# The attention's query load as two transfers of 64 rows in place of one that reads its source twice

## The chip, the cores and the metric

The kernel runs on one core of one Trainium2 chip. Its time is the device time of one execution in microseconds (us); before the change it is 2788.62 us, the median of three runs (2783.65 to 2796.56). A core has five engines with a queue of instructions each: TensorE (PE, with its weight loads shown apart as PEld), VectorE (DVE), ScalarE (ACT), GpSimd (POOL) and SyncE (SP). Transfers between the core's memory (SBUF) and the device's memory are issued by an engine's queue and carried out by the core's 16 DMA engines. Here SP and POOL issue them: the profile calls SP's transfers hardware_dynamic (q1) and POOL's software_dynamic (q0).

## The reference

One layer of a hybrid decoder is run for a prompt of 2048 tokens behind 16 meta tokens, and for 8 x 8 sample tokens with a paged cache of 512 keys each. One input projection gives q, k and v for 8 heads of width 64 and the inputs of a recurrent branch. Attention weights come from a product over the keys behind a position, taken from the query backwards:

```python
z = jnp.einsum('bqhd,bkhd->bhqk', q, k) * (HEAD_DIM ** -0.5) + bias
mask = k_pos[None, :] < q_pos[:, None]
log_keep = jnp.where(mask, jax.nn.log_sigmoid(-z), 0.0)
suffix = lax.cumsum(log_keep, axis=3, reverse=True) - log_keep
w = jnp.where(mask, jnp.exp(jax.nn.log_sigmoid(z) + suffix), 0.0)
out = jnp.einsum('bhqk,bkhd->bqhd', w, v)
...
mixed = jnp.concatenate([attn, lru * jax.nn.gelu(gate)], axis=-1) @ w_out
x = x + rmsnorm(mixed, g_mix_post)
u = jax.nn.relu(rmsnorm(x, g_mlp_pre) @ w_up)
x = x + rmsnorm((u * u) @ w_down, g_mlp_post)
```

## The kernel before, in words

All values are float32. Each operand of a large matrix product is split into a rounded part and the rest (names with `hi` and `lo`), and a product is the sum of three matrix products: lines L181 to L183 where the weights stand still in the array, L213 to L215 where the activations do. Weights come in tiles of 512 KB (`wraw`, two buffers), loaded by SP (L149) and split by ACT (L158) and DVE (L159).

The prompt is worked in four blocks of 512 tokens (`s` from 0 to 3). First comes the input projection of block 0 with the sample tokens, and then, beside the following input projections, the attention of the sample tokens (`sample_attn`: cache pages are gathered by POOL at L831, PE uses them at L854 and L883). Then the input projections of blocks 1 to 3, and after them the output projection and the MLP of blocks 0 to 3. The prompt's attention (`attn`) is side work that lasts into the MLP of block 2 (PE's last L702 stands at 2126.7 us): a planner (`Work`) cuts it into small steps and puts a few of them on PE's queue after every few matrix products of the main work, by a table of rates. PE's order is written out this way by hand. The other engines' instructions are put in order by a scheduler. Each queue runs in order, so an instruction that waits holds up what stands behind it.

The input projection stores its queries, split, in the device's memory as `qd[s]` with the shape [8 heads, 64, 2, 512] (L604), its keys as `kd` (L550) and its values as `vd` (L556). The attention of block `s` takes the heads one after the other. For each head, `head` loads the queries into the tile `q` (128 partitions, 2 x 512 elements: 4 KB per partition, two buffers). The 64 rows of the head stand in it twice, in partitions 0 to 63 and again in 64 to 127, because the keys beside it hold their rounded part in the upper 64 partitions and the rest in the lower 64. This load is the line L667, issued by POOL. `head` also loads the block's last 128 keys and values (`kvt`, L671 and L672), and `kv_load` the others in groups (`kv`: L684, L685 and L688 for the first group, L691 and L692 for the others). The two buffers of `q` also serve the sample attention's weights (`wt`, L871).

A step of attention is then: logits on PE (L702, from `kv` or `kvt` and `q`), two sigmoids on ACT (L640, L641), a scan and a product on DVE (L645 or L648, L652), transposes on PE (L712), a split on ACT and DVE (L719, L720, L723, L724; for the 16 meta keys POOL clears the tile first at L718), and the product with the values on PE (L734, L736). A head's result is summed into a tile with the tag `pb` (L744, L745) and stored in `md` by SP (L746). The scan's results use the same two `pb` buffers.

POOL's queue holds, besides the loads, the gate's polynomial in the input projection (L524 to L528, L454), small copies for the convolution (L499, L502) and the inverse roots of the norms (L237).

POOL's transfers announce their landing through eight semaphores, DMASW0 to DMASW7, taken in turn. The transfer that takes a semaphore again waits until the transfer eight places earlier has landed.

Of the kernel before, what the change touches and what calls it, by code (L numbers as in the profile page):

```python
# [20 lines left out]
HD = 64  # L21
NMETA = 16
SB = 512
# [61 lines left out]
def _program(tc, I, O, NSB, NSC):  # L85

    nc = tc.nc
# [16 lines left out]
    def T(p, shape, dt, tag, bufs=1):  # L104
        uid[0] += 1
        return p.tile(shape, dt, name=f"{tag}_{uid[0]}", tag=tag, bufs=bufs)
# [162 lines left out]
    qd = [dt([NH, HD, 2, SB], F32, name=f"qd{s}") for s in range(NSB)]  # L269
# [386 lines left out]
    def attn(s, K):  # L656
# [4 lines left out]
        def keys(h, a, n):  # L661
            return kd[h].rearrange("e p n -> (e p) n")[:, a:a + n]

        def head(h):
            if h < NH and h not in heads:
                q = T(att, [P, 2, SB], F32R, "q", 2)
                nc.gpsimd.dma_start(q.rearrange("p e n -> p (e n)"),  # L667
                                    qd[s][h].rearrange("p e n -> p (e n)").unsqueeze(0).to_broadcast([2, HD, 2 * SB]))
                kt = T(att, [P, 256], F32R, "kvt", 3)
                k0 = SB * s + 3 * P  # L670
                nc.gpsimd.dma_start(kt[:, 0:P], keys(h, NMETA + k0, P))  # L671
                nc.gpsimd.dma_start(kt[:, P:2 * P], vd[h, :, k0:k0 + P])  # L672
                live["kvt"] += 1
                heads[h] = {"q": q, "kt": kt, "carry": [None] * 4, "out": None}
            return heads.get(h)
# [72 lines left out]
        def s_items():  # L748

            for n, (h, g) in enumerate(groups):  # L750
                H = head(h)
                if g == s:
                    head(h + 1) if live["kvt"] < 3 else None
                while live["kv"] > 2:
                    yield None
                kv_load(n)
                kv_load(n + 1)
                head(h)
                kvt = kvs.pop(n)
                if g == 0:  # L760
# [533 lines left out]
```

## Time and profile before

| | |
|---|---|
| median of three runs | 2788.62 us (2783.65 to 2796.56) |
| the profiled execution's own time | 2790.22 us |
| its span, first to last instruction | 2788.3 us |
| mean clock granted to PE | 0.985 |
| DVE, ACT, POOL busy | 65%, 52%, 18% of the span |
| bytes moved | 368.23 MB, 132 GB/s |
| by SP's queue and POOL's queue | 287.35 MB and 78.52 MB |

How to read it: a time in a row is counted from the start of the span. "Landing" is the time from the issue of a transfer until its semaphore is complete. In a timeline, a bracket at the end of a row tells how long the engine was idle before it and what ended the wait. The chain of waits is the work that ended last, followed back from the last instruction of the span. The granted clock (PEclk) is 1.00 when PE runs at full speed.

### The profile page before, as it was taken

The page shows a single profiled execution, that of the slowest core. Times are in us where ns is not written, and L with a number is a line of the kernel's source. Part 1 is how long each engine was busy: PE and PEld are TensorE (multiplying, and loading weights), DVE is VectorE, ACT ScalarE, POOL GpSimd, SP SyncE. Part 2 cuts the span into 40 slices and gives each one's busy share as a digit, 9 for nine tenths or more (in the row PEclk, how much of TensorE's full clock was granted, in tenths as well). Part 3 has the DMA queues.
Part 4 walks back from the last instruction along what each step waited for, and adds up shares of the span by engine and source line. Part 5 has one row for each costly group of instructions (what it writes and reads, how often), then busy time and mean ns, then how long its engine had stood idle before and what let it go on. Part 6 is the DMA issues. An engine that isn't in the chain of part 4 may idle for free.

```text
span 2788.3 us, 36998 instructions
## 1 busy us (share of the span) xinstructions
PE 2688.2 (96%) x13804; PEld 2219.4 (80%) x13804; DVE 1814.3 (65%) x2790; ACT 1451.6 (52%) x2426; POOL 515.5 (18%) x711
## 2 busy tenths in 40 slices
PE   8999988998899999999999999999999999999998
PEld 6886766777688888887788888878888887998996
DVE  5456364686777777788867777798686436433434
ACT  6556364575665655565555555665555234332332
POOL 5336361341211101112110001120000002000002
PEclk9999998999999999999999999999999999999999
DMA  4465855467534433345443333454333334322223
GB/s 161 134 208 189 261 152 171 134 169 221 166 92 128 119 115 106 106 138 154 154 110 115 103 111 103 138 162 143 105 96 104 112 119 144 99 84 77 83 84 113
DMA packets 177316, 368.23 MB, mean 132 GB/s; under 512 B 49153, under 2 KB 79361, under 8 KB 177137
## 3 DMA queue, kind: packets, MB, share of 16 engines
q1 hardware_dynamic: 103792, 287.35, 32.2%
q0 software_dynamic: 73344, 78.52, 11.3%
q8 instruction: 109, 1.79, 0.3%
q14 instruction: 71, 0.57, 0.1%
HBM read 305.51 MB, written 60.04 MB: 131 GB/s over the span
## 4 chain that ended last, share of the span: by engine, by line
PE 80%; DVE 7%; DMA 5%; POOL 3%; issue 3%; ACT 2%; SPq 0%; POOLq 0%; DVEq 0%; ACTq 0%
PE D L181 11%; PE D L183 11%; PE D L182 11%; PE D L213 10%; PE D L214 10%; PE D L215 10%; PE T L712 4%; PE T L702 4%; PE O L734 2%; PE O L736 2%; DVE wlo L159 1%; DMA md<-pb 1%; DVE pb L648 1%; POOL rstd L237 1%; DMA q<-qd 1%
## 5 line engine op out<-in xcount | busy, mean ns | idle before, releaser
L159 DVE TENSOR_TENSOR wlo<-wraw,whi 128x1024 fp32r<-128x1024 f32 x368 | 464.2, 1261 | 496.1 <-ACT whi L158 495.8
L181 PE MATMUL D<-ahi,whi 128*128 128x512 f32 (+3 forms) x1920 | 709.2, 369 | 0.0
L183 PE MATMUL D<-ahi,wlo 128*128 128x512 f32 (+3 forms) x1920 | 686.3, 357 | 2.0 <-DVE wlo L159 2.0
L182 PE MATMUL D<-alo,whi 128*128 128x512 f32 (+3 forms) x1920 | 685.0, 357 | 2.8 <-DVE alo L1017 1.5
L158 ACT CAST whi<-wraw 128x1024 fp32r<-128x1024 f32 x368 | 386.6, 1050 | 485.5 <-PE D L214 282.8
L213 PE MATMUL D<-whi,uh 128*128 128x512 f32 x1024 | 418.1, 408 | 0.0
L183 PEld LDWEIGHTS D<-ahi,wlo 128*128 128x128 f32 x1920 | 364.8, 190 | 53.2 <-DVE wlo L159 2.9
L181 PEld LDWEIGHTS D<-ahi,whi 128*128 128x128 f32 x1920 | 365.2, 190 | 51.9 <-issue 8.7
L214 PE MATMUL D<-whi,ul 128*128 128x512 f32 x1024 | 405.2, 396 | 0.0
L215 PE MATMUL D<-wlo,uh 128*128 128x512 f32 x1024 | 404.3, 395 | 0.0
L182 PEld LDWEIGHTS D<-alo,whi 128*128 128x128 f32 x1920 | 365.7, 190 | 45.5 <-DVE alo L1017 1.7
L640 ACT ACTIVATE keep<-T,nbias 128x512 f32<-128x512 f32 (+6 forms) x352 | 209.7, 596 | 241.7 <-PE T L702 234.6
L648 DVE TENSOR_TENSOR_SCAN pb<-keep,carry 128x513 f32<-128x513 f32 (+1 forms) x228 | 270.3, 1186 | 71.9 <-ACT keep L640 69.9
L724 DVE TENSOR_TENSOR wtl<-T,wth 128x512 fp32r<-128x512 f32 (+1 forms) x320 | 191.0, 603 | 73.7 <-ACT wth L723 72.6
L723 ACT CAST wth<-T 128x512 fp32r<-128x512 f32 (+1 forms) x320 | 166.1, 523 | 127.6 <-PE T L712 122.7
L215 PEld LDWEIGHTS D<-wlo,uh 128*128 128x128 f32 x1024 | 192.7, 188 | 46.7
L213 PEld LDWEIGHTS D<-whi,uh 128*128 128x128 f32 x1024 | 192.9, 188 | 39.9 <-DVE uf L1032 0.4
L214 PEld LDWEIGHTS D<-whi,ul 128*128 128x128 f32 x1024 | 193.3, 189 | 38.6
L652 DVE TENSOR_TENSOR beta<-beta,pb 128x512 f32<-128x512 f32 (+7 forms) x360 | 208.2, 578 | 0.0
L641 ACT ACTIVATE beta<-T,bias 128x512 f32<-128x512 f32 (+6 forms) x352 | 208.2, 591 | 0.0
L712 PE MATMUL T<-ident,beta 128*128 128x128 f32 (+1 forms) x1216 | 193.7, 277 | 14.1 <-ACT beta L641 7.6
L702 PE MATMUL T<-kv,q 128*128 128x512 f32 (+5 forms) x640 | 180.4, 364 | 10.3 <-ACT beta L641 4.4
(235 smaller groups left out, 3600.0 us busy)
## 6 DMA issues: line engine op xcount, KB each, us to landing
wraw<-in_w_up SPq DMA_DIRECT2D x128, 512.0 KB, 3.5
wraw<-in_w_down SPq DMA_DIRECT2D x128, 512.0 KB, 3.5
wraw<-in_w_in SPq DMA_DIRECT2D x64, 512.0 KB, 3.9
q<-qd POOLq DMA_DIRECT2D x32, 512.0 KB, 16.9
wraw<-in_w_out SPq DMA_DIRECT2D x32, 512.0 KB, 3.5
kv<-kd POOLq DMA_DIRECT2D x48, 256.0 KB, 4.1
kv<-vd POOLq DMA_DIRECT2D x48, 256.0 KB, 4.2
y<-in_x_prompt SPq DMA_DIRECT2D x16, 512.0 KB, 5.6
```

The costliest lines, as they stand in the source:

```text
L158: nc.scalar.copy(hi, r)
L159: nc.vector.tensor_tensor(lo, r, hi.bitcast(F32), op=ALU.subtract)
L181: nc.tensor.matmul(o, whi[:, k, :], ahi(k, a, b), start=(k == 0), stop=False)
L182: nc.tensor.matmul(o, whi[:, k, :], alo(k, a, b), start=False, stop=False)
L183: nc.tensor.matmul(o, wlo[:, k, :], ahi(k, a, b), start=False, stop=(k == KC - 1))
L213: nc.tensor.matmul(o, h, whi[:, kk, :], start=st, stop=False)
L214: nc.tensor.matmul(o, l, whi[:, kk, :], start=False, stop=False)
L215: nc.tensor.matmul(o, h, wlo[:, kk, :], start=False, stop=sp)
L640: nc.scalar.activation(keep[:, o:512], S, AF.Sigmoid, bias=nbias, scale=-0.125)
L648: nc.vector.tensor_tensor_scan(pb[:, o:513][:, ::-1], kr, kr, 1.0 if carry is None else carry, op0=ALU.mult, op1=ALU.bypass)
L702: nc.tensor.matmul(o, H["q"][:, e, i * P:(i + 1) * P], kap, start=(e == 0), stop=(e == 1))
L712: nc.tensor.transpose(t[0:kn, i * P:(i + 1) * P], w[:, c0:c0 + kn], ident)
```

## The change

The transfer at L667 had a source that names the head's 64 rows of 4 KB twice: a first dimension of 2 with a step of zero, then 64 rows. It is replaced by two transfers (L668) of the same 64 rows each, one into partitions 0 to 63 and one into 64 to 127. The bytes, the tile and its two buffers stay the same. There are 32 heads in all, so 32 transfers of 512 KB become 64 of 256 KB.

```diff
         def head(h):
             if h < NH and h not in heads:
                 q = T(att, [P, 2, SB], F32R, "q", 2)
-                nc.gpsimd.dma_start(q.rearrange("p e n -> p (e n)"),
-                                    qd[s][h].rearrange("p e n -> p (e n)").unsqueeze(0).to_broadcast([2, HD, 2 * SB]))
+                for r in range(2):
+                    nc.gpsimd.dma_start(q[HD * r:HD * r + HD].rearrange("p e n -> p (e n)"), qd[s][h].rearrange("p e n -> p (e n)"))
                 kt = T(att, [P, 256], F32R, "kvt", 3)
```

The orders of PE, DVE, ACT and SP stay as they were, instruction by instruction; only POOL's queue changes. The first place is the first query load of block 0, in the middle of the gate's polynomial and just ahead of the last cache page (L831). In brackets stand the semaphores that a row waits for. Before:

```order
L525 TENSOR_SCALAR gt_3699<-gt_3699 128x512 [waits Pool_49]
L667 DMA q_3925<-qd_78 128x1x1024 [waits DMAHW4_49]
L526 TENSOR_TENSOR gt_3699<-gt_3699,g_3697 128x512 [waits Pool_49]
L528 TENSOR_TENSOR gt_3699<-gt_3699,g_3697 128x512 [waits Activation_49]
L454 TENSOR_TENSOR ii_3765<-ii_3765,xc_3661 128x512 [waits Activation_49]
L831 DMA kv_3835<-in_cache_v,ix_199 128x512 [waits DMASW7_49,DMASW6_49,PE_49]
```

The same place after the change:

```order
L525 TENSOR_SCALAR gt_3699<-gt_3699 128x512 [waits Pool_49]
L668 DMA q_3925<-qd_78 64x1024 [waits DMAHW4_49]
L526 TENSOR_TENSOR gt_3699<-gt_3699,g_3697 128x512 [waits Pool_49]
L668 DMA q_3925<-qd_78 64x1024
L528 TENSOR_TENSOR gt_3699<-gt_3699,g_3697 128x512 [waits Activation_49]
L454 TENSOR_TENSOR ii_3765<-ii_3765,xc_3661 128x512 [waits Activation_49]
L831 DMA kv_3835<-in_cache_v,ix_199 128x512 [waits DMASW7_49,DMASW6_49,PE_49]
```

The second half stands one instruction behind the first, and the cache page stands one instruction later.

The second place is a later head of block 0, on POOL's queue: its query load, its `kvt` and its group of `kv`. Before, seven transfers make a head:

```order
L667 DMA q_5182<-qd_78 128x1x1024 [waits DMASW3_49,PE_49]
L671 DMA kvt_5184<-kd 128x128 [waits DMASW4_49,PE_49]
L684 DMA kv_4833<-kd 128x400 [waits DMASW5_49,PE_49]
L685 DMA kv_4833<-vd 128x384 [waits DMASW6_49]
L686 MEMSET kv_4833 128x128
L672 DMA kvt_5184<-vd 128x128 [waits DMASW7_49]
L688 DMA kv_4833<-vmd 16x128 [waits DMASW0_49,Pool_49]
L688 DMA kv_4833<-vmd 16x128 [waits DMASW1_49]
```

After the change there are eight:

```order
L668 DMA q_5187<-qd_78 64x1024 [waits DMASW0_49,PE_49]
L668 DMA q_5187<-qd_78 64x1024 [waits DMASW1_49]
L671 DMA kvt_5190<-kd 128x128 [waits DMASW2_49,PE_49]
L684 DMA kv_4838<-kd 128x400 [waits DMASW3_49,PE_49]
L685 DMA kv_4838<-vd 128x384 [waits DMASW4_49]
L686 MEMSET kv_4838 128x128
L672 DMA kvt_5190<-vd 128x128 [waits DMASW5_49]
L688 DMA kv_4838<-vmd 16x128 [waits DMASW6_49,Pool_49]
L688 DMA kv_4838<-vmd 16x128 [waits DMASW7_49]
```

With eight transfers to a head, each waits for the semaphore of the same transfer of the head before.

The third place is the only one where two instructions change places, on POOL's queue in an input projection (the copy at 558.30 us of the profile). Before:

```order
L718 MEMSET wth_5101 128x512 [waits PE_49]
L528 TENSOR_TENSOR gt_5043<-gt_5043,g_5041 128x512 [waits Activation_49]
L667 DMA q_5464<-qd_78 128x1x1024 [waits DMAHW7_49,DMASW2_49,PE_49]
L502 COPY convc_240<-xp_5140 128x3 [waits Activation_49]
L454 TENSOR_TENSOR ii_5112<-ii_5112,xc_4994 128x512 [waits Activation_49]
L499 COPY xp_5268<-convc_240 128x3 [waits DVE_49,Pool_49]
```

After:

```order
L718 MEMSET wth_5106 128x512 [waits PE_49]
L528 TENSOR_TENSOR gt_5048<-gt_5048,g_5046 128x512 [waits Activation_49]
L668 DMA q_5470<-qd_78 64x1024 [waits DMAHW7_49,DMASW0_49,PE_49]
L668 DMA q_5470<-qd_78 64x1024 [waits DMASW1_49]
L454 TENSOR_TENSOR ii_5117<-ii_5117,xc_4999 128x512 [waits Activation_49]
L502 COPY convc_240<-xp_5145 128x3
L499 COPY xp_5274<-convc_240 128x3 [waits DVE_49,Pool_49]
```

The product L454 now stands ahead of the small copy L502 there.

## The prediction

> **What bounds the kernel now.** I read the page first, then PE's time by stretches, then who it waited for, then the chain of waits, and last the transfers. The page's first part says that PE is the bound:
>
> ```profile
> PE 2688.2 (96%) x13804; PEld 2219.4 (80%) x13804; DVE 1814.3 (65%) x2790; ACT 1451.6 (52%) x2426; POOL 515.5 (18%) x711
> ```
>
> Some 100 us are left in which PE stands still. The stretches show where (PE busy is the second number, and the last three are granted clock, DMA share and GB/s):
>
> ```profile
> 395.00:800.00 405.00, 354.54 (x1680) 281.70 (x1680) 275.34 (x460) 238.60 (x421) 108.06 (x159) 0.92 0.57 163
> 800.00:2788.00 1988.00, 1961.67 (x9808) 1644.99 (x9806) 1325.02 (x2006) 988.24 (x1651) 216.55 (x338) 1.00 0.38 115
> ```
>
> From 395 to 800 us, where block 0's attention runs beside the input projections and the first output projection, PE idles 50 us and has a clock of 0.92. Behind 800 us it idles 26 us in 1988 at full clock. The query load's line within the first stretch counts 13 of the 32 loads:
>
> ```profile
> L667 POOL DMA_DIRECT2D q<-qd x13: 798/817/911, 401.7 to 765.7; - x13
> ```
>
> So the 19 others run beside a PE that hardly waits. What the change can give lies in the first stretch. PE's waits there, the longest first (total, times, longest):
>
> ```profile
> PE O L883 <- DMA kv<-in_cache_v,ix: 7.7, 1, 7.7
> PE T L712 <- ACT beta L641: 7.6, 2, 4.8
> PE T L702 <- DMA q<-qd: 6.0, 1, 6.0
> ```
>
> One wait names the query load itself. The chain of waits names a transfer as the last releaser in each of these places (start, duration):
>
> ```profile
> 408.55 11.47 DMA kv<-in_cache_v,ix
> 426.47 20.01 DMA q<-qd
> 470.96 12.12 DMA vd<-vst
> 496.57 11.24 DMA md<-pb
> 558.93 8.36 DMA md<-gt
> 621.89 9.47 DMA md<-pb
> 643.25 8.69 DMA out_v_prompt<-sf
> ```
>
> The profile's list of transfers shows that several of these are slow for their kind (KB each, median us to landing):
>
> ```profile
> wraw<-in_w_up SPq DMA_DIRECT2D x128, 512.0 KB, 3.5
> q<-qd POOLq DMA_DIRECT2D x32, 512.0 KB, 16.9
> kv<-kd POOLq DMA_DIRECT2D x48, 256.0 KB, 4.1
> ...
> vd<-vst SPq DMA_DIRECT2D x12, 512.0 KB, 7.8
> ...
> md<-pb SPq DMA_DIRECT2D x32, 128.0 KB, 3.8
> ...
> kv<-in_cache_v,ix POOLq DMA_INDIRECT x32, 5.1
> ```
>
> A query load takes 16.9 us, a weight tile of the same 512 KB 3.5. Why is read from a stretch in which a query load (issued at 514.7) moves almost alone:
>
> ```profile
> 519.00:522.00 3.00, 3.00 (x22) 2.55 (x21) 1.91 (x3) 2.11 (x4) 0.00 (x0) 1.00 0.14 52
> ```
>
> It moves 52 GB/s with a DMA share of 0.14, and 0.14 x 16 is 2.2 engines. At 52 GB/s its 524 KB take 10 us, and the rest of the 16.9 is start, end and company. The old source's first dimension is 2. I take it that a load is shared out over the engines by that dimension, two engines here. So the load is slow itself and, for some 15 us, fills two of the engines that every other transfer needs too. While the load of 462.9 us was in flight, these landed:
>
> ```profile
> vd<-vst SPq DMA_DIRECT2D x2, 512.0 KB, 10.5
> ...
> md<-pb SPq DMA_DIRECT2D x1, 128.0 KB, 11.9
> kvt<-kd POOLq DMA_DIRECT2D x1, 64.0 KB, 12.4
> ```
>
> The `kvt` load, 64 KB, took as long as the rest of the query load ahead of it; the `md` store took three times its median.
>
> **The change part by part.**
>
> *The halves' landing.* No row shows a POOL load of 64 rows. The nearest below is `kv<-kd` with the same 256 KB in 128 rows, 4.1 us; the far end is the old load, 16.9. I take 5 us for both halves (4.1, and the second issued 0.6 us later with some company), since 64 rows are a first dimension like `kv`'s 128, not like the old 2.
>
> The Trainium skill (DMA: Bandwidth & Descriptors, section "Why a DMA increments its semaphore by 16 and not by 1") says that a copy runs on the largest number of engines up to 16 that divides the slowest dimension of both sides: 2 for the old source and 16 for 64 rows. The 0.14 agrees for the old; no run yet shows the new. The same page (section "Anatomy of one DMA") puts a load at about 2.0 us plus bytes over 436 GB/s. By that the old load would be an estimated 3.2 us and two halves 2.6 each, so that splitting would only add a fixed cost and the sum would be nothing; the measured 16.9 says that this formula does not hold for the old shape.
>
> *POOL's extra issue.* Rows of POOL's timeline, the query load of the second head with what stands around it, and the next:
>
> ```profile
> 426.47 0.83 POOL L667 DMA_DIRECT2D q<-qd  x1 [4.77 <-issue]
> 427.29 0.56 POOL L684 DMA_DIRECT2D kv<-kd  x1
> ...
> 438.12 0.80 POOL L667 DMA_DIRECT2D q<-qd  x1 [8.24 <-PE T L702]
> ```
>
> One issue of 0.83 becomes two of about 0.56: 0.3 us a head, 10 us over 32 heads, on an engine that is 18% busy and stands 8.24 us waiting for PE ahead of the next such load. On the path: 0. Without that cover it would be 0.3 us for each of 13 heads before 800 us, 4 us. At the first load the cache page L831 comes later by one issue, 0.56 us; there too POOL waits for ACT in between, so I count 0. The exchanged L502 comes some 2 us later, one time, ahead of an L499 that waits for DVE anyway: 0.
>
> *The semaphores.* A second half waits for the transfer eight places ahead, now the same half of the head before, landed long ago: 0. Behind it on POOL would stand the `kv` loads, L718 and the gate's products, for which PE and ACT wait. One such wait existed and should go:
>
> ```profile
> 419.67 0.55 POOL L685 DMA_DIRECT2D kv<-vd  x1 [5.27 <-DMA q<-qd]
> ```
>
> *Term 1, the query wait at 440 us.* PE's rows with the waits (idle before, releaser), and the half-speed stretches that follow them, PEclk third from the end:
>
> ```profile
> 420.06 0.65 PE L883 MATMUL O<-kv,q 128*32 128x128 f32 x8 [7.69 <-DMA kv<-in_cache_v,ix]
> ...
> 446.61 0.66 PE L702 MATMUL T<-kvt,q 128*128 128x128 f32 x2 [6.01 <-DMA q<-qd]
> ```
>
> ```profile
> 420.60:425.10 4.50, 4.50 (x21) 2.71 (x18) 0.84 (x1) 1.62 (x3) 0.98 (x2) 0.50 0.29 67
> 446.60:452.30 5.70, 5.69 (x16) 4.76 (x17) 2.29 (x8) 2.04 (x6) 0.00 (x0) 0.50 0.53 169
> 485.20:490.00 4.80, 4.80 (x15) 3.50 (x16) 4.57 (x11) 3.38 (x8) 1.34 (x2) 0.50 0.83 227
> 513.30:517.30 4.00, 3.92 (x14) 3.05 (x15) 3.04 (x7) 1.53 (x3) 0.81 (x1) 0.50 0.64 183
> 653.80:657.20 3.40, 3.36 (x8) 2.71 (x9) 1.92 (x2) 1.39 (x3) 1.60 (x3) 0.51 0.50 139
> ```
>
> Each long wait is followed by work at a clock of 0.50, half of which is lost time. The load was issued at 426.47 and PE asked for it at 440.6, 14.1 us later; with 5 us it is there in time. Saved: 6.0 and half of 5.7, 8.9 us.
>
> *Term 2, the cache page at 412 us.* It was issued at 408.55 behind the first query load and landed after 11.47. With the usual 5.1 it lands 6.4 earlier, leaving 1.3 of the 7.69. Half of the 4.5 us behind it goes too: 8.6 us. If it keeps its old landing, 0; if the wait goes wholly, 9.9.
>
> *Term 3, the second-hand waits.* PE's later waits that the chain leads back to a slow transfer:
>
> ```profile
> 485.16 0.48 PE L712 MATMUL T<-ident,beta 128*128 128x128 f32 x1 [4.80 <-ACT beta L641]
> 509.56 0.66 PE L261 MATMUL T<-ident,y 128*128 128x128 f32 x4 [2.85 <-DVE wtl L724]
> 583.63 0.44 PE L712 MATMUL T<-ident,beta 128*128 128x128 f32 x2 [2.80 <-ACT beta L641]
> 633.11 0.63 PE L702 MATMUL T<-kv,q 128*128 128x400 f32 x2 [1.42 <-DVE wtl L724]
> 653.84 0.79 PE L734 MATMUL O<-wth,kv 128*128 128x512 f32 x1 [2.98 <-DVE wth L720]
> ```
>
> With half of the stretches behind them they come to 4.80 + 2.4, 2.85 + 2.0, 2.80, 1.42 and 2.98 + 1.7, together 21 us. I take a third, 7.0 us: in the stretch from 485.2 DVE is busy 4.57 of 4.80 us, so there PE would soon wait for DVE, and a DMA share of 0.83 leaves the stores other company than the query load.
>
> *Sum.* 8.9 + 8.6 + 7.0 = 24.5 us. The profiled execution took 2790.22 us and would take 2765.7; it lies 1.6 above the median of 2788.62, which becomes **2764**. With all of term 3 and 9.9 in term 2 the gain is 39.8 us, 2749.
>
> **The rivals.**
>
> *The waits pass on.* Only term 1 holds, and the cache page and the stores stay slow, because DMA shares of 0.57 to 0.83 come from all the traffic and not from the query load. For it: DVE's 4.57 of 4.80. Against it: the 64 KB `kvt` load at 12.4 us. The time would be 2788.6 - 8.9 = 2780.
>
> *The change doesn't do what it says.* The 64 rows too run on few engines, and both halves land after 15 us or more. The 14.1 us at 440 stay too short and nothing is gained: 2789. For it: no row shows 64 rows. Against it: `kv`'s 4.1. The formula of the Trainium skill's page cited above would give no gain either, by another way.
>
> *Slower.* POOL becomes the late one: the second half waits on its queue for a semaphore of a load not yet landed, and the `kv` loads and L718 behind it come late to PE. At most that is an issue and a landing, 0.8 + 4.1 = 4.9 us, for each of the 13 heads before 800 us: 64 us against the 24.5 gained, 2828. It decides from 2 us a head that reach PE. For it: the 5.27 us above show that such a wait occurs. Against it: it was one wait, made by the slow load, and POOL is 18% busy.
>
> **How the numbers follow.** Forecast 0.74 (the 2-engine share and the wait that names the load are both in the trace); the waits pass on 0.15; doesn't do what it says 0.06; slower 0.05. What a measurement of this kernel can tell from no change is about 0.5%, 13.9 us, or 2774.7; the three runs themselves lie 13 us apart. The forecast is faster (0.74), the next two rivals are the same (0.21), the last is slower (0.05). The range goes from 2749, all of the terms, to 2780, the first rival, and leaves out the other two.
>
> **What would show it.** After the change the query load should land in about 5 us, PE's wait for `q` at L702 should be gone, the cache page should land near 5 us, and the stretch from 395 to 800 us should be some 24 us shorter with a clock above 0.95; behind it, nothing changes. Waits of POOL for semaphores of its own loads would speak for the slower rival. I am wrong if the halves land after more than 14 us, or if they land fast and the stretch is not shorter by 9 us at least.

## The result, and the profile after

The changed kernel takes 2754.15 us (median of five runs, 2751.61 to 2756.03), the one before 2789.36 us (five runs, the three known before and two more, 2783.65 to 2796.56). The ratio is 0.9871, with a 95% interval of 0.9853 to 0.9889: 35 us less, where 24.5 were forecast.

The page after shows PE's busy time 13 us lower, though it does the same 13804 products, and the span 36.2 us lower:

```profile
span 2752.1 us, 37027 instructions
...
PE 2675.1 (97%) x13804; PEld 2210.4 (80%) x13804; DVE 1816.8 (66%) x2790; ACT 1451.1 (53%) x2426; POOL 522.2 (19%) x743
```

PE's order is the same in both kernels, so the two traces can be laid side by side at the same products. Three stretches are used from here on. Stretch I goes from a product shortly ahead of the first query load's issue to the end of the half-speed work behind PE's wait for `q`; II from there to the end of the half-speed work behind the wait for L734; III goes on to the product that stands at 1000.1 us before the change. A fourth row goes on from there, nearly to the end. The columns are start:end, duration, then busy time and number of instructions of PE, PEld, DVE, ACT and POOL, granted clock, DMA share and GB/s. Before:

```profile
395.10:452.60 57.50, 43.80 (x237) 32.20 (x236) 27.32 (x46) 27.63 (x48) 19.65 (x26) 0.85 0.63 170
452.60:657.60 205.00, 186.12 (x868) 148.88 (x867) 137.47 (x227) 124.73 (x215) 65.35 (x92) 0.95 0.56 159
657.60:1000.10 342.50, 324.61 (x1557) 267.29 (x1556) 262.80 (x440) 205.29 (x365) 51.81 (x96) 0.96 0.49 140
1000.10:2774.10 1774.00, 1759.09 (x8820) 1476.59 (x8819) 1163.56 (x1742) 867.64 (x1440) 184.35 (x279) 1.00 0.37 114
```

And the same products after the change:

```profile
394.10:433.80 39.70, 38.77 (x237) 28.96 (x236) 26.15 (x44) 27.39 (x48) 20.36 (x29) 1.00 0.79 228
433.80:617.40 183.60, 178.25 (x867) 143.74 (x867) 141.71 (x230) 124.94 (x217) 66.05 (x99) 1.00 0.63 179
617.40:959.30 341.90, 324.15 (x1556) 266.61 (x1555) 262.70 (x439) 205.11 (x365) 54.61 (x105) 0.97 0.49 141
959.30:2734.20 1774.90, 1761.82 (x8820) 1478.85 (x8819) 1163.29 (x1742) 867.58 (x1440) 188.07 (x293) 1.00 0.37 114
```

Stretch I is 17.8 us shorter, II 21.4, III 0.6, the fourth 0.9 longer. What is left of the 36.2 lies ahead of 395 us (1.0 less) and behind the fourth row (3.7 more), where no query load stands; what made the end longer was not followed up. The clock in I and II rises from 0.85 and 0.95 to 1.00, and these two hold 12.9 of the 13.1 us that PE is busy less. PE waits no longer for `q`, and 0.9 us in place of 7.7 for the cache page. Its longest waits from 395 to 800 us are now others:

```profile
PE T L261 <- DVE y L1003: 5.5, 2, 4.6
PE D L213 <- ACT ahi L951: 3.8, 1, 3.8
PE T L702 <- ACT beta L641: 3.4, 1, 3.4
```

All three stand in stretch III. One wait is still put down to `q`. Its row in the timeline, with the weight load ahead of it, shows how such a name is to be taken:

```profile
565.21 0.19 PEld L734 LDWEIGHTS O<-wth,kv 128*128 128x128 f32 x1 [1.60 <-DVE wth L720]
565.21 0.50 PE L734 MATMUL O<-wth,kv 128*128 128x512 f32 x1 [1.46 <-DMA q<-qd]
```

The product L734 does not read `q`. Its weight load, in the same instant, is put down to DVE's `wth` (L720), which the product does read; the landing of `q` only fell on the same moment.

The halves land in a median of 5.2 us, 8.5 at most:

```profile
q<-qd POOLq DMA_DIRECT2D x64, 256.0 KB, 5.2
```

A stretch in which the two halves issued at 725.7 us are nearly alone (the last numbers are granted clock, DMA share and GB/s) shows the engines at work:

```profile
727.20:729.00 1.80, 1.03 (x6) 0.79 (x4) 1.80 (x3) 1.49 (x3) 0.00 (x0) 0.80 1.10 255
```

255 GB/s and a DMA share of about 1 stand where 52 GB/s and 0.14 stood: all of the engines, not two. That is what the Trainium skill (DMA: Bandwidth & Descriptors, section "Why a DMA increments its semaphore by 16 and not by 1") says of 64 rows, and the trace agrees. The packets tell it again. Before and after:

```profile
DMA packets 177316, 368.23 MB, mean 132 GB/s; under 512 B 49153, under 2 KB 79361, under 8 KB 177137
```

```profile
DMA packets 149155, 368.11 MB, mean 134 GB/s; under 512 B 20992, under 2 KB 51200, under 8 KB 148976
```

28161 small packets are gone. If 14 idle engines got one small packet for each of the 64 rows that the two others carried, 32 loads made 32 x 14 x 64 = 28672 of them; the 32 new transfers bring 32 x 16 = 512, one for each engine. The difference, 28160, is one less than the number found.

### The profile page after: what moved, and what is told of

Read it like the earlier page. It is cut to its first block, busy times and chain, and to the rows that moved or that the text cites. A ratio compares the mean times of both kernels' runs of the same rounds, so it can differ in the third digit from the quotient of the medians.

```text
span 2752.1 us, 37027 instructions
## 1 busy us (share of the span) xinstructions
PE 2675.1 (97%) x13804; PEld 2210.4 (80%) x13804; DVE 1816.8 (66%) x2790; ACT 1451.1 (53%) x2426; POOL 522.2 (19%) x743
## 4 chain that ended last, share of the span: by engine, by line
PE 83%; DVE 7%; POOL 3%; DMA 3%; issue 2%; ACT 2%; SPq 0%; POOLq 0%; DVEq 0%; ACTq 0%
PE D L181 12%; PE D L183 12%; PE D L182 11%; PE D L213 11%; PE D L214 11%; PE D L215 11%; PE T L712 4%; PE T L702 4%; PE O L734 2%; PE O L736 2%; DVE wlo L159 1%; POOL rstd L237 1%; DVE pb L648 1%; PE O L219 1%; PE O L218 1%
## 5 line engine op out<-in xcount | busy, mean ns | idle before, releaser
L158 ACT CAST whi<-wraw 128x1024 fp32r<-128x1024 f32 x368 | 386.5, 1050 | 469.2 <-PE D L214 285.9
L213 PEld LDWEIGHTS D<-whi,uh 128*128 128x128 f32 x1024 | 193.1, 189 | 39.8 <-DVE uf L1032 0.4
```

Source lines behind the costliest of these rows:

```text
L158: nc.scalar.copy(hi, r)
L213: nc.tensor.matmul(o, h, whi[:, kk, :], start=st, stop=False)
```

## The experiments

All have the kernel before as their base, and only the query load is edited unless said otherwise. The theory is that of the prediction: the old load runs on two engines, is slow for that, and takes these two from everything else. Before 395 us, where no query load stands, the runs differ by some us (stretch I begins between 389.4 and 400.9), so places are compared by the stretches and wholes by the ratio.

### One transfer of the usual shape

```diff
-    qd = [dt([NH, HD, 2, SB], F32, name=f"qd{s}") for s in range(NSB)]
+    qd = [dt([NH, 2 * HD, 2, SB], F32, name=f"qd{s}") for s in range(NSB)]
...
-                    nc.sync.dma_start(qd[s][2 * c:2 * c + 2, :, e, :].rearrange("h p n -> (h p) n"), t[:, o0:o0 + SB].bitcast(F32))
+                    for hh in range(2):
+                        for r in range(2):
+                            nc.sync.dma_start(qd[s][2 * c + hh, HD * r:HD * r + HD, e, :], t[HD * hh:HD * hh + HD, o0:o0 + SB].bitcast(F32))
...
+                nc.gpsimd.dma_start(q.rearrange("p e n -> p (e n)"), qd[s][h].rearrange("p e n -> p (e n)"))
```

> The queries are stored twice in the device's memory (eight store transfers of 64 rows in place of two of 128 rows per pair of heads, 8.4 MB more in all), and a head's load is ONE transfer of 128 rows of 4 KB without a repeated dimension. Theory (a load is shared out over the DMA engines by its source's first dimension, and 2 means two engines): the load lands in 4 to 6 us as the two halves do (5.2), though it is one transfer; time near the changed kernel's 2754, or up to 10 us above it for the extra stores. Rival (two transfers help because the second runs beside the first, not because of the shape): one transfer of 512 KB still lands after 13 us or more, and the time is 2785 or above.

Measured: 2764.89 us, ratio 0.9929 (0.9909 to 0.9948). The load's line, and stretches II and III:

```profile
q<-qd POOLq DMA_DIRECT2D x32, 512.0 KB, 3.8
```

```profile
436.90:620.20 183.30, 178.23 (x868) 143.78 (x867) 141.66 (x230) 125.02 (x217) 62.20 (x92) 1.00 0.65 191
620.20:969.50 349.30, 324.06 (x1556) 266.92 (x1555) 263.65 (x439) 204.80 (x365) 49.86 (x97) 0.96 0.49 144
```

One transfer of 512 KB lands in 3.8 us, faster than a half did. So the number of transfers is not what helps; the repeated dimension was what hurt. Stretch II is as short as in the changed kernel. The whole is 10.7 us above the changed kernel's 2754.15, and by the ratio more, so it misses the 10 us that were allowed for the stores. Stretch I is 2.8 us longer than there (42.5, of which PE waits 2.3 for the cache page in place of 0.9), III 7.4, with longer waits of PE for ACT (6.7 us for L951's `ahi`, against 3.8, and 3.4 for weights that L158 splits). The stores of the queries, 96 more on SP's queue, are the only other edit; how they lead to these waits was not followed up.

### The first two loads alone, and all but these

```diff
+                if s == 0 and h < 2:
+                    for r in range(2):
+                        nc.gpsimd.dma_start(q[HD * r:HD * r + HD].rearrange("p e n -> p (e n)"), qd[s][h].rearrange("p e n -> p (e n)"))
+                else:
+                    nc.gpsimd.dma_start(q.rearrange("p e n -> p (e n)"),
+                                        qd[s][h].rearrange("p e n -> p (e n)").unsqueeze(0).to_broadcast([2, HD, 2 * SB]))
```

> Only the first two loads (block 0, heads 0 and 1) are two transfers of 64 rows; the other 30 are as before. Theory (the terms of the sum add up, place by place): the query wait and the cache page's wait go, 8.9 + 8.9 us, and the later second-hand waits (21 us) stay: 2771, ratio 0.9935. Rival (the whole gain follows from the start of the attention, the later waits vanish only because PE, ACT and DVE stand differently to each other after it): near 2754. Rival (it all comes from company in the later loads): near 2789.

Measured: 2768.29 us, ratio 0.9933 (0.9917 to 0.9950). The profiled execution is the longest of the five, 2780.58 us, and comes late to stretch I. Stretches I and II:

```profile
400.90:441.10 40.20, 38.76 (x237) 28.97 (x236) 26.17 (x44) 27.39 (x48) 20.20 (x28) 1.00 0.74 218
441.10:646.20 205.10, 185.77 (x868) 148.62 (x867) 138.53 (x230) 124.84 (x216) 65.45 (x92) 0.95 0.59 164
```

The complement has `if s > 0 or h >= 2` in its first line.

> The complement: the first two loads as before, the other 30 as two transfers of 64 rows. Theory: the second-hand waits go, the first two stay: 21 us saved, 2768, ratio 0.9925. Rival (everything from the first two loads): near 2789. Rival (the waits pass on): 2780 or above.

Measured: 2771.45 us, ratio 0.9945 (0.9929 to 0.9962). Stretches I and II:

```profile
393.00:452.70 59.70, 44.28 (x237) 32.57 (x236) 28.71 (x48) 29.02 (x50) 20.42 (x28) 0.83 0.64 172
452.70:636.60 183.90, 178.38 (x867) 143.67 (x866) 140.60 (x227) 124.58 (x216) 65.85 (x99) 1.00 0.62 175
```

The terms are separate. The first two loads are worth stretch I and nothing else (57.5 to 40.2, II unchanged at 205.1); the others are worth stretch II and nothing else (205.0 to 183.9, I not shorter at 59.7). The wholes agree: the ratios fall short of 1 by 0.0067 and 0.0055, together 0.0122, where the changed kernel has 0.0129. The second is less than the 0.0075 expected. The rival by which the later waits only vanish because of what happened at the start has fallen: they vanish without it. So has the rival by which the waits are passed on.

### The loads of blocks 2 and 3 alone

The first line is `if s >= 2`.

> Only the loads of blocks 2 and 3 (16 of 32, all behind 1050 us, where PE hardly waits) are two transfers of 64 rows. Theory: their landing falls from 16.9 to about 5 us and the time stays: 2787 to 2791, ratio 1.000. Rival (a fast load is worth something wherever it stands, by less company for the weights): half of the gain, 2772.

Measured: 2788.54 us against 2787.08, ratio 1.0011 (0.9999 to 1.0023): nothing, as expected. Where PE hardly waits, a fast load is worth nothing, although it still frees the engines: the page counts 35072 packets under 512 B, 14081 fewer than before, about half of what the changed kernel saves. The landing of these loads, expected at about 5 us, is not told by this trace.

### Two halves that keep the repeated dimension

```diff
+                for e in range(2):
+                    nc.gpsimd.dma_start(q[:, e, :], qd[s][h][:, e, :].unsqueeze(0).to_broadcast([2, HD, SB]))
```

> Two transfers per head as in the changed kernel, and the same bytes, but cut by columns: each takes half of each row (2 KB) and still reads its 64 source rows twice, so the first dimension stays 2. Theory (two engines for such a transfer): slow, 64 packets on each engine. If both halves use the same two engines the landing stays above 13 us and the time is 2785 or above; if the second takes two other engines, four work at a time, the landing is 8 to 11 us and the time lies between, 2760 to 2780. Rival (cutting in two is what helps, whatever the shape): landing near 5 us, time near 2754.

Measured: 2758.14 us, ratio 0.9912 (0.9893 to 0.9931). The load's line:

```profile
q<-qd POOLq DMA_DIRECT2D x64, 256.0 KB, 10.4
```

A stretch in which both halves issued at 728.7 us are alone, and then stretches I and II:

```profile
732.00:736.00 4.00, 2.02 (x8) 1.50 (x9) 3.16 (x9) 0.97 (x2) 0.00 (x0) 0.83 0.29 87
```

```profile
391.20:435.30 44.10, 41.24 (x237) 30.35 (x236) 25.42 (x44) 27.58 (x48) 21.72 (x29) 0.92 0.76 199
435.30:621.40 186.10, 178.73 (x867) 143.48 (x866) 141.62 (x230) 124.59 (x216) 69.65 (x99) 1.00 0.66 179
```

0.29 x 16 is 4.6 engines, and 87 GB/s lie between 52 and 255: the share is twice that of the old load. The packets say that each transfer had two engines:

```profile
DMA packets 210595, 368.34 MB, mean 134 GB/s; under 512 B 78336, under 2 KB 108544, under 8 KB 210416
```

That is 57344 small ones more than in the changed kernel, which has as many transfers, and 57344 is 64 x 14 x 64. So two transfers of two engines each ran at once on different engines, as the second branch of the theory had it. That makes a ladder of 2, about 4 and 16 engines with landings of 16.9, 10.4 and 5.2 us. The gain does not climb it evenly: with four engines stretches I and II already give 13.4 + 18.9 = 32.3 of the 39.2 us. The whole came out a little below the range expected for this rung, 2760 to 2780. The kernel before ran at 2785.58 us beside it, though: by the ratio, 0.9912 of 2788.62 us, it would be 2764, which is inside.

### Four quarters

```diff
+                for r in range(4):
+                    p0 = HD // 2 * r
+                    nc.gpsimd.dma_start(q[p0:p0 + HD // 2].rearrange("p e n -> p (e n)"), qd[s][h][p0 % HD:p0 % HD + HD // 2].rearrange("p e n -> p (e n)"))
```

> Four transfers of 32 rows per head, 128 in all, each 128 KB. Theory (what counts is that all engines share the load; POOL has room): the landing of the last quarter is 5 to 6 us after the first issue, POOL issues 1.1 us more per head beside its waits, and the time is that of the changed kernel, 2754, within 5 us. Rival (each further transfer costs POOL's queue an issue and a semaphore wait that reaches PE): 13 heads by 1.1 us or more, 2768 and above.

Measured: 2748.34 us, ratio 0.9873 (0.9857 to 0.9890), which is the changed kernel's 0.9871 (the kernel before ran at 2785.58 us beside it). A quarter lands in a median of 3.2 us. Stretches I and II:

```profile
389.40:429.30 39.90, 38.77 (x238) 28.96 (x237) 26.18 (x44) 27.39 (x48) 23.18 (x35) 1.00 0.79 223
429.30:613.10 183.80, 178.34 (x868) 143.60 (x866) 141.78 (x230) 124.89 (x217) 72.37 (x113) 1.00 0.63 180
```

In II POOL is busy 6.3 us more than in the changed kernel, and the stretch is 0.2 us longer. The issues of further transfers hide behind POOL's waits, at twice their number as well. This was the mechanism of the slower rival, and these runs show no price of it.

### Rows that do not divide evenly

```diff
+                for r in range(2):
+                    for a, b in ((0, 62), (62, 64)):
+                        nc.gpsimd.dma_start(q[HD * r + a:HD * r + b].rearrange("p e n -> p (e n)"), qd[s][h][a:b].rearrange("p e n -> p (e n)"))
```

> Four transfers per head: 62 rows, 2 rows, 62 rows, 2 rows. Of the numbers up to 16, 2 is the largest that divides 62. Theory A (the engines of a transfer are the largest number up to 16 that divides its first dimension): two engines for each, 31 packets on each for the long ones; landing 8 to 11 us, time between, 2758 to 2780. Theory B (a plain transfer is dealt out in shares of a sixteenth whatever its rows, and only the repeated dimension of the old source made it two engines): landing about 5 us and time as with four quarters, near 2754.

Measured: 2747.04 us, ratio 0.9864 (0.9848 to 0.9881). The loads' lines:

```profile
q<-qd POOLq DMA_DIRECT2D x64, 248.0 KB, 4.1
...
q<-qd POOLq DMA_DIRECT2D x64, 8.0 KB, 3.9
```

Theory B held: 62 rows land in 4.1 us, no later than 64 (5.2). The packets of the quarters and of this kernel, which has as many transfers, differ by 1024 small ones:

```profile
DMA packets 150180, 368.13 MB, mean 134 GB/s; under 512 B 22016, under 2 KB 52224, under 8 KB 150000
```

```profile
DMA packets 151204, 368.13 MB, mean 134 GB/s; under 512 B 23040, under 2 KB 53248, under 8 KB 151024
```

That is 64 x (2 + 14): 62 rows on 16 engines with four places each leave two places empty, 2 rows leave 14. On two engines with 31 rows each, 62 rows would leave 14 x 31 = 434 places empty for each of the 64 transfers. The Trainium skill's rule (the same page and section) would give two engines for 62; the page also tells of an exception, by which some plain copies of POOL's queue are dealt out over 16 engines in shares rounded up, and the trace agrees with the exception.

## Why the prediction was right, and where a term was too small

*The cause.* Two engines, by the repeated first dimension: held. The shares of 0.14, 0.29 and 1.10 and the packets show it, and the one transfer of 128 rows lands in 3.8 us.

*The halves' landing.* Taken at 5, measured 5.2. With 35 us less, the rivals that gave no gain have fallen, the one by which splitting only adds a fixed cost too.

*Terms 1 and 2.* 17.5 us were forecast for what is now stretch I, and it is 17.8 us shorter. PE's two products that had waited stand here, with 0.87 us of wait in place of 7.69, and none in place of 6.01:

```profile
412.30 0.43 PE L883 MATMUL O<-kv,q 128*32 128x128 f32 x8 [0.87 <-DMA kv<-in_cache_v,ix]
...
430.60 0.33 PE L702 MATMUL T<-kvt,q 128*128 128x128 f32 x2
```

The second product, 0.66 us at the half clock before, takes 0.33 us: the half-speed stretches went with the waits, as the sum had it. Its two parts came out too: PE stands idle 12.8 us less in stretch I, where the two terms have 12.4 us of waits, and is busy 5.0 us less, where they have 5.1 for the half clock.

*Term 3.* This is the term that was too small. The full price of the second-hand waits was 21 us, of which the prediction took a third, 7.0; stretch II is 21.4 us shorter, so all of it came. With it the sum is 39.8 us at most, and I and II gave 39.2. The first reason given for the cut was that DVE was busy 4.57 of 4.80 us behind the wait at 485 us, and that PE would meet it there. Rows of ACT and DVE ahead of that point, before the change, tell where these 4.57 us came from:

```profile
479.15 0.59 ACT L561 COPY sf<-D 128x512 f32<-128x512 f32 x1 [5.31 <-DMA out_v_prompt<-sf]
480.72 1.23 DVE L159 TENSOR_TENSOR wlo<-wraw,whi 128x1024 fp32r<-128x1024 f32 x1 [5.99 <-ACT whi L158]
483.15 0.59 ACT L564 CAST vst<-D 128x512 fp32r<-128x512 f32 x1 [2.47 <-DMA vd<-vst]
```

ACT waited for two slow stores to land, its weight split L158 stood behind the first of them, and DVE waited 5.99 us for that. The nearly full 4.8 us were the work that had piled up meanwhile, and were read as a steady load. Over all of stretch II DVE is busy 137 of 205 us before and 142 of 184 after.

The second reason was a DMA share of 0.83 there, by which the stores would have company enough without the query load. But the stores became faster. These are medians to landing within stretch II, in us; the second column is from the kernel with four quarters, as the changed kernel's trace does not tell most of them:

| transfer | before | quarters |
|---|---|---|
| `vd<-vst` (store, SP) | 9.4 | 5.8 |
| `out_v_prompt<-sf` (store, SP) | 7.3 | 3.7 |
| `qd<-sl` (store, SP) | 10.1 | 3.7 |
| `md<-pb` (store, SP) | 6.9 | 5.8 |
| `wraw<-in_w_in` (load, SP) | 5.3 | 3.6 |
| `kvt<-kd` (load, POOL) | 12.1 | 3.3 |

The changed kernel's trace does tell the waits for them in stretch II: DVE's for `md<-pb` fall from 11.4 to 0.3 us in all, ACT's for `out_v_prompt<-sf` from 11.1 to 5.3 and for `vd<-vst` from 3.7 to 1.1. The DMA share meanwhile rises from 0.56 to 0.63.

*What cost nothing.* POOL's busy time rose by 6.7 us (515.5 to 522.2; 10 forecast for the extra issues), and from 395 to 800 us PE waits for none of POOL's instructions. The issue of both halves takes 1.05 us, and the `kv` load that had waited 5.27 us for the first query load's semaphore now follows without a wait (its neighbour rows, after the change):

```profile
412.62 0.57 POOL L684 DMA_DIRECT2D kv<-kd  x1
413.19 0.55 POOL L685 DMA_DIRECT2D kv<-vd  x1
...
415.58 1.05 POOL L668 DMA_DIRECT2D q<-qd  x2 [0.36 <-issue]
```

*What stayed.* Behind stretch II nothing was gained, and the sum had counted no wait there. The waits in III, which the chain before had partly led back to a store (`x1d<-y`), remain.

## What to carry to other kernels

A transfer that takes several times as long as others of its size, at a small and steady DMA share, is worth a look at the first dimension of its access pattern on both sides, a repeated one above all, before its bytes; here it ran on two engines. Its price was not only who waited for it: transfers that shared its engines or stood behind it in its queue were slow too. So follow the chain of waits to their landings. Here these waits went at full price, and the discount taken for a busy engine was wrong: before taking one, look whether the engine is busy over the whole stretch. A few microseconds of a full engine just behind a wait can be a backlog, and say nothing then of the room it has.

## What was not expected of the hardware

That two transfers of two engines each would run on different ones, at 87 GB/s together, had been open. A POOL load of 62 rows is dealt out over all 16 engines, with small packets in the empty places. And most of the gain needed only the step from two engines to about four: 32.3 of 39.2 us in stretches I and II, at a landing that is still 10.4 us. A load behind it in the queue shows steps of the same kind: in stretch II `kvt<-kd` lands in 12.1 us beside two engines at work, 6.3 beside about four, and 3.3 with the quarters.
